# A hybrid decoder layer on one core: setup products as steps beside the first layer, exponents ordered behind copies of turned keys, attention rows' halves ordered behind the third convolution tile

## Chip, core and metric

The kernel runs on one core of a Trainium2 chip. The metric is the device time of one execution in microseconds (us). The engines are TensorE (PE, matrix products and transposes), VectorE (DVE), ScalarE (ACT), GpSimd (POOL) and SyncE (SP, which issues DMAs only). DMAs are also issued from ACT's and POOL's queues.

## What is computed

One layer for a prompt of 512 tokens and 8 samples of 8 tokens, 576 columns together:

```python
h = x + 0.5 * swiglu(rmsnorm(x, ffn1_norm), ...)          # D 1024, D_FF 2816
xn = rmsnorm(h, mix_norm)
z, xbc, dt, q, k, v, f, g_ssd, g_att = split_combined(xn @ w_in)
y_ssd = ssd_branch(z, xbc, dt, state_conv, state_ssm)     # causal conv of 4 taps on 3072 channels, scan, gate, norm
c = cumsum(logf)                                          # per head, over cached pages and new tokens
y_att = softmax(q k^T / 8 + c_q - c_k) v                  # 16 heads, 4 key heads; samples also see 2048 cached tokens
h = h + (sigmoid(g_ssd) * (y_ssd @ w_ssd_proj) + sigmoid(g_att) * (y_att @ w_attn_proj)) @ w_out
y = h + 0.5 * swiglu(rmsnorm(h, ffn2_norm), ...)
```

The inputs that the change touches are `state_conv` (the last three rows before the convolution, of each sample), `cache_logf` (logs of the forget gates in 160 pages, of which `page_table` names 128), and `state_ssm` (the scan's state).

## The kernel before

**Products.** Activations lie with features on partitions and the 576 tokens as columns, worked on in two halves of 288. Each fp32 product is made of three products in a faster format (`mm3`): a weight tile is split into a high part (`whi`, a copy on ACT, L173) and a low part (`wlo`, a difference on DVE or POOL, L174), and the activations into `xh` and `xl` in the same way; PE adds high by high (L208), high weight by low activation (L209) and low weight by high activation (L210). So a tile of 128 outputs by 288 columns over 1024 features is 24 matmuls. Weights come in stages of 512 KB on SP's queue, four of them in rotation.

**Order.** Each engine carries out its instructions in a fixed order. A scheduler sets it when the program is built: it goes by the order of the code, by a simulated time, and by `soon()`, which moves what is inside it ahead. During attention PE's order is written by hand (`manual_schedule`).

**The first layer.** `ffn` runs over 22 feature tiles in two parts (12 and 10): per tile four half products (96 matmuls), and after each part 8 output tiles. After each of these 38 steps it calls a generator named `beside`, which puts in a piece of other work. In the kernel before, that generator is `turns(4)`: after four steps, each step loads 256 KB of the scan's state on SP (L375), transposes it on PE (`tr`, L376), copies it on ACT (`hT`, L378) and stores it to DRAM (`hTD`).

**Setup.** In the code ahead of the first layer stand two small pieces. One loads the convolution rows (`sc`, L510), transposes them in 24 pieces (L515), copies them (`scT`, L516) and stores them to `scD` (L517). The other gathers the cached logs by page (`lg`, L524), runs 16 scans along the pages on DVE (`pf`, L529), collects their ends (`tot`, L531), multiplies them on PE by a matrix that sums over the earlier pages (L535), copies the result (`st`, L537), subtracts it in 16 instructions on POOL (L540), and stores the outcome to `pastD` in 32 DMAs on ACT's queue (L546). The state loads of `turns` take the memory that this piece leaves.

**Attention.** The loop takes 37 steps. In a step one key tile row of the prompt's pair of heads (`cur`) and one quarter of a sample's cached keys (`new`) are worked on. The pair's rows end in an exponent (`L`, ACT, L867), the first step of a pair with 512 columns, the others with fewer. The sample's keys are transposed on PE (L924) and copied on ACT (`kT`, L926); PE then multiplies them by the queries (L935). The results for the samples are collected in `ys` (DVE, L997) and at the end copied by POOL into the eight attention rows `qy` (L1114).

**Convolution.** `conv_tile` is called for the tiles B, C and X0 to X3 of a group of heads (`group_in`). It copies the stored rows into `xr` on POOL (L1129), runs the two half products, evicts them on DVE (L1133, L1138, L1140), transposes the last rows on PE into the free end of the second half's bank (L1146), copies that on ACT (`tt`, L1148), stores it, and works out the convolution (`kf`: ACT L1157, DVE L1159), its tanh (ACT, L1160) and the outputs (DVE). From here on two banks of PSUM serve the products. After the six tiles come the halves of the eight attention rows: `yh` on ACT (L217) and `yl` on DVE (L218), called from L1185, and then the projection of attention.

## Time and profile before

| | us |
|---|---|
| median of 3 runs | 1887.17 (1885.02, 1887.17, 1891.32) |
| the profiled execution | 1890.57 |
| its span in the trace | 1888.4 |
| PE busy | 1834.7 |
| DVE busy | 1062.6 |
| ACT busy | 746.2 |
| POOL busy | 606.5 |

The span is the time from the first to the last instruction of the profiled execution; what lies around it is 2.2 us. The page gives for each engine its busy time, which is a share of the span, and for a wait the engine and line that waited, the engine or DMA that ended the wait, and the total, the number and the longest. Numbers of buffers are left out of names in these views (`acc`, `whi`); in the rows of an order they stand behind the name. The granted clock is TensorE's, as a share of full speed.

### The profile page before, as it was taken

Reading aid. Unit: us, or ns where it says so; the run is one execution under the profiler, and the core shown is the slowest. Engines: PE = TensorE matmul, PEld = TensorE weight load, DVE = VectorE, ACT = ScalarE, POOL = GpSimd, SP = SyncE. Lnnn points to the kernel's source line nnn. Section 1 sums busy time; section 2 is a strip of 40 time slices with the busy share of each in tenths; the row PEclk is TensorE's granted clock in tenths of the full one; section 3 lists DMA queues with packets and bytes.
Section 4 is the critical chain, followed back from the end, with each engine's and each line's share of the span. In section 5 each row is a group of like instructions: output and inputs, shape, how many; then the busy total and the mean of one; then the engine's idle time right before and its main releaser. Section 6 shows DMA issues by size and latency. Waiting matters only on the chain.

```text
span 1888.4 us, 38769 instructions
## 1 busy us (share of the span) xinstructions
PE 1834.7 (97%) x15335; PEld 1729.5 (92%) x15335; DVE 1062.6 (56%) x2309; ACT 746.2 (40%) x1555; POOL 606.5 (32%) x681
## 2 busy tenths in 40 slices
PE   7999999999999999999999999999999999999998
PEld 7999999999889787888899898888989999999998
DVE  4544234434425677777655968787695544444442
ACT  4233223334323545545335645454433333223322
POOL 0432003322322344443323735656553332002210
PEclk9999999999999999999999999999999999999999
DMA  5453443445525678775456545354463444444432
GB/s 154 107 147 124 134 124 112 124 146 142 140 79 167 184 223 228 233 217 156 117 144 189 151 113 149 98 152 143 134 210 90 118 130 133 144 132 125 117 119 67
DMA packets 297722, 269.71 MB, mean 143 GB/s; under 512 B 55068, under 2 KB 262092, under 8 KB 297388
## 3 DMA queue, kind: packets, MB, share of 16 engines
q1 hardware_dynamic: 229712, 184.16, 34.9%
q10 hardware_dynamic: 57828, 46.10, 7.9%
q0 software_dynamic: 10000, 36.97, 6.3%
q8 instruction: 121, 1.98, 0.5%
q14 instruction: 61, 0.50, 0.1%
HBM read 223.72 MB, written 38.73 MB: 139 GB/s over the span
## 4 chain that ended last, share of the span: by engine, by line
PE 83%; DVE 7%; DMA 3%; ACT 3%; issue 2%; POOL 1%; ACTq 1%; SPq 0%; DVEq 0%; POOLq 0%
PE acc L208 16%; PE acc L209 16%; PE acc L210 15%; PE pv L209 8%; PE pv L208 8%; PE pv L210 7%; PE tr L935 2%; PE tr L924 1%; PE mm L861 1%; DMA ab<-cumD 1%; PE pv L892 1%; DVE kf L1159 1%; PE mm L879 1%; PE pv L973 1%; PE tr L376 1%
## 5 line engine op out<-in xcount | busy, mean ns | idle before, releaser
L173 ACT ACTIVATE whi<-stage 128x512 fp32r<-128x512 f32 (+2 forms) x474 | 294.7, 622 | 713.0 <-PE acc L209 605.2
L208 PE MATMUL acc<-xh,whi 128*128 128x288 f32 x1792 | 542.3, 303 | 8.4 <-ACT tt L1148 3.6
L209 PE MATMUL acc<-xl,whi 128*128 128x288 f32 x1792 | 533.8, 298 | 0.0
L210 PE MATMUL acc<-xh,wlo 128*128 128x288 f32 x1792 | 533.0, 298 | 0.0
L174 DVE TENSOR_TENSOR wlo<-stage,whi 128x512 fp32r<-128x512 f32 (+1 forms) x373 | 260.7, 699 | 268.1 <-ACT whi L173 251.1
L208 PEld LDWEIGHTS acc<-xh,whi 128*128 128x128 f32 x1792 | 339.5, 189 | 15.7 <-ACT tt L1148 7.7
L209 PEld LDWEIGHTS acc<-xl,whi 128*128 128x128 f32 x1792 | 339.7, 190 | 2.9 <-issue 2.7
L210 PEld LDWEIGHTS acc<-xh,wlo 128*128 128x128 f32 x1792 | 338.9, 189 | 1.1 <-issue 0.5
L174 POOL TENSOR_TENSOR wlo<-stage,whi 128x512 fp32r<-128x512 f32 (+1 forms) x101 | 138.4, 1370 | 287.7 <-ACT whi L173 275.5
L341 POOL TENSOR_TENSOR u<-u,s 128x288 f32<-128x288 f32 x88 | 81.5, 927 | 437.2 <-DVE u L340 379.8
L208 PE MATMUL pv<-xh,whi 128*128 128x288 f32 (+1 forms) x720 | 214.2, 298 | 1.7 <-ACT xh L220 1.5
L209 PE MATMUL pv<-xl,whi 128*128 128x288 f32 (+1 forms) x720 | 213.1, 296 | 0.0
L210 PE MATMUL pv<-xh,wlo 128*128 128x288 f32 (+1 forms) x720 | 212.6, 295 | 0.0
L208 PEld LDWEIGHTS pv<-xh,whi 128*128 128x128 f32 (+1 forms) x720 | 135.3, 188 | 2.3 <-ACT xh L220 1.8
L209 PEld LDWEIGHTS pv<-xl,whi 128*128 128x128 f32 (+1 forms) x720 | 135.1, 188 | 1.3
L210 PEld LDWEIGHTS pv<-xh,wlo 128*128 128x128 f32 (+1 forms) x720 | 135.2, 188 | 0.2
L208 PE MATMUL pv<-hh,whi 128*128 128x288 f32 x352 | 105.7, 300 | 0.0
L343 POOL TENSOR_TENSOR hl<-u,hh 128x288 fp32r<-128x288 f32 x88 | 79.4, 904 | 80.4 <-ACT hh L342 80.4
L209 PE MATMUL acc<-hl,whi 128*128 128x288 f32 x352 | 104.1, 296 | 0.0
L208 PE MATMUL acc<-hh,whi 128*128 128x288 f32 x352 | 104.1, 296 | 0.0
L209 PE MATMUL pv<-hl,whi 128*128 128x288 f32 x352 | 104.1, 296 | 0.0
L210 PE MATMUL acc<-hh,wlo 128*128 128x288 f32 x352 | 104.1, 296 | 0.0
(364 smaller groups left out, 3618.0 us busy)
## 6 DMA issues: line engine op xcount, KB each, us to landing
stage<-in_w_in_dram SPq DMA_DIRECT2D x52, 512.0 KB
stage<-in_ffn_w_up_dram SPq DMA_DIRECT2D x44, 512.0 KB
stage<-in_ffn_w_gate_dram SPq DMA_DIRECT2D x43, 512.0 KB
stage<-in_ffn_w_down_dram SPq DMA_DIRECT2D x40, 512.0 KB
h<-in_state_ssm_dram SPq DMA_DIRECT2D x64, 256.0 KB
hTD<-hT ACTq DMA_DIRECT2D x32, 256.0 KB
pb<-pastD SPq DMA_DIRECT2D x32, 256.0 KB
ab<-cumD SPq DMA_DIRECT2D x32, 256.0 KB
```

The source lines that it names most:

```text
L173: act(hi, view, AF.Copy)
L174: e.tensor_tensor(lo, view, hi.bitcast(F32), ALU.subtract)
L208: mm(out, lhsT=hi, rhs=a, start=first and i == 0, stop=False)
L209: mm(out, lhsT=hi, rhs=b, start=False, stop=False)
L210: mm(out, lhsT=lo, rhs=a, start=False, stop=last and i == n - 1)
L341: G.tensor_tensor(u, u, sil[half], ALU.mult)
L343: G.tensor_tensor(hl[:, hs(half)], u, hh[:, hs(half)].bitcast(F32), ALU.subtract)
L376: nc.tensor.transpose(ps[:, b * P:(b + 1) * P], h0[:, b, :], ident)
L861: mm(s[:, :n], lhsT=q, rhs=ks[2 * self.p + e][:, :n], start=hl == 0, stop=hl == 1)
L879: nc.tensor.transpose(t[:, j * P:(j + 1) * P], lt[:, j * P:(j + 1) * P], ident)
L892: mm(self.ob[o:o + 32, i * P:(i + 1) * P], lhsT=vtok[j][:, v0:v0 + 32], rhs=self.pts[e][:, j * P:(j + 1) * P], start=j == 0, stop=j == i)
L935: mm(s[kv * 32:(kv + 1) * 32, :], lhsT=self.q(kv), rhs=self.kT[kv // 2], start=True, stop=True)
```

## The change

It has three parts. Two tiles of the setup code become steps of a new generator `aside`, which runs beside the first layer: the loads of the convolution rows at the first call, their transposes after two more, then the gather and the scans, and after two further calls the matrix product, the subtractions and the stores; the state's turning follows as `turns(1)`, and its loads are issued up to three steps ahead. In attention, the exponents of a pair's first step are ordered behind both copies of the turned keys of the same step. After attention, the copies into the attention rows and their halves move behind `group_in`, where each of them is ordered behind an instruction of the third convolution tile, X0: POOL's copy behind X0's copy of the stored rows, ACT's `yh` behind X0's tanh, DVE's `yl` behind X0's last output. The tile `ys` moves to another pool for that. `behind` adds an order between two instructions, which the scheduler keeps.

```diff
+    def behind(later, first):
+        tc.add_manual_dep(later.ins, first.ins.name, ..., reason="order")
...
 def turns(wait):
+            tiles = []
             for t in range(16):
                 for h in range(2):
-                    h0 = tl(sp_, [P, 4, P], tag="h0", bufs=4)
-                    nc.sync.dma_start(out=h0, in_=ap3(A["state_ssm"][0], *place(h, t)))
+                    for n in range(len(tiles), min(2 * t + h + 3, 32)):
+                        tiles.append(tl(sp_, [P, 4, P], tag="h0", bufs=4))
+                        nc.sync.dma_start(out=tiles[n], in_=ap3(A["state_ssm"][0], *place(n % 2, n // 2)))
+                    if t + h == 0:
+                        yield
+                    h0 = tiles[2 * t + h]
...
+        def aside():
+            with pool("rows", side="right", reuse_waits="tile") as su:
+                sc = tl(su, [24, CONV], tag="sc")
...
+                yield
+                yield
+                scT = tl(su, [P, 24, 24], tag="scT")
...
+            with pool("lg", side="right", reuse_waits="tile") as lp:
...
+                for _ in range(2):
+                    yield
+                t = sm()
+                mm(t[:, :16], lhsT=page, rhs=tot, start=True, stop=True)
...
+            yield from turns(1)
...
-        ffn(nrm1, cg, A["ffn1_w_up"][0], A["ffn1_w_down"][0], hts, done1, turns(4))
+        ffn(nrm1, cg, A["ffn1_w_up"][0], A["ffn1_w_down"][0], hts, done1, aside())
...
-        ys = tl(ap, [P, 2, 4, NS], tag="ys")
+        ys = tl(yp, [P, 2, 4, NS], tag="ys")
...
-                    act(lt[:, :n], lt[:, :n], AF.Exp, bias=mn, scale=-1.0, accum_out=sum_)
+                    self.exps.append(act(lt[:, :n], lt[:, :n], AF.Exp, bias=mn, scale=-1.0, accum_out=sum_))
...
                     with soon():
-                        act(self.kT[p], t, AF.Copy)
+                        copy = act(self.kT[p], t, AF.Copy)
+                    for x in exps:
+                        behind(x, copy)
...
-                    new.turn_keys(jq)
+                    new.turn_keys(jq, cur.exps if jq == 0 else ())
...
-        for p in range(2):
-            for g in range(4):
-                G.tensor_copy(yt[p * 4 + g][:, NP:], ys[:, p, g, :])
...
-            yhl = [hilo(yhp, y, "yh", "yl", bufs=8) for y in yt]
+            yhl = []
+            for n, y in enumerate(yt):
+                c = G.tensor_copy(y[:, NP:], ys[:, n // 4, n % 4, :])
+                hi = tl(yhp, [P, NT], F32R, tag="yh", bufs=8)
+                lo = tl(yhp, [P, NT], F32R, tag="yl", bufs=8)
+                h = act(hi, y, AF.Copy)
+                for x, first in zip((c, h, V.tensor_tensor(lo, y, hi.bitcast(F32), ALU.subtract)), convs[2]):
+                    behind(x, first)
+                yhl.append((hi, lo))
```

How it moves instructions shows at three places. The first is on PE, in the first layer, around the transposes of the convolution rows; before:

```order
L208 MATMUL acc_706<-xh_203,whi_672 128x288
L209 MATMUL acc_706<-xl_204,whi_672 128x288
L210 MATMUL acc_706<-xh_203,wlo_673 128x288
L515 MATMUL tr_335<-ident_76,sc_330 128x24 x12
L515 MATMUL tr_349<-ident_76,sc_330 128x24 x12
L208 MATMUL acc_706<-xh_216,whi_672 128x288
L209 MATMUL acc_706<-xl_217,whi_672 128x288
L210 MATMUL acc_706<-xh_216,wlo_673 128x288
```

The same place of the program on PE with the change, where the line of the transposes is L530:

```order
L212 MATMUL acc_746<-xh_229,whi_712 128x288
L213 MATMUL acc_746<-xl_230,whi_712 128x288
L214 MATMUL acc_746<-xh_229,wlo_713 128x288
L530 MATMUL tr_777<-ident_76,sc_484 128x24 x12
L530 MATMUL tr_791<-ident_76,sc_484 128x24 x12
L212 MATMUL pv_845<-xh_138,whi_837 128x288
L213 MATMUL pv_845<-xl_139,whi_837 128x288
```

Before, the transposes stand inside the second feature tile's second product, behind 186 matmuls of 288 columns; now they stand between the third and the fourth tile, behind 288. The product of the totals (L535, now L551) has 480 such matmuls ahead of it instead of 312, and the first state transposes (L376, now L385) 734 instead of 555; between the two are 254 instead of 243. On DVE, with the change, the scans (L543) and what stands behind them read as follows.

```order
L344 TENSOR_TENSOR u_940<-pv_915,rbc_262 128x288
L543 SCALAR_TENSOR_TENSOR pf_814<-cst_75,lg_812 128x128 x16
L178 TENSOR_TENSOR wlo_1056<-stage_1051,whi_1055 128x512
L344 TENSOR_TENSOR u_970<-acc_945,rbc_262 128x288
L178 TENSOR_TENSOR wlo_1060<-stage_1053,whi_1059 128x512
L545 COPY tot_831<-pf_814 128x16
```

Before, an eviction (`u`) stood between the fourteenth and the fifteenth scan; now all sixteen stand together, ahead of a weight's low part, which PE first reads at its matmul number 435.

The second place is on ACT, at the first step of a pair in attention; before (`Ls` and `Ln` are the samples' exponents, `L` the pair's, `kT` the copies of turned keys):

```order
L951 ACTIVATE Ls_7380,sums_7389<-Ls_7380,mxs_6934 128x512
L952 ACTIVATE Ln_7387,sums_7389<-Ln_7387,mxs_6934 128x64
L867 ACTIVATE L_7418,sum_7421<-L_7418,mn_7419 128x512
L867 ACTIVATE L_7429,sum_7432<-L_7429,mn_7430 128x512
L926 ACTIVATE kT_7458<-tr_7459 128x512
L926 ACTIVATE kT_7465<-tr_7466 128x512
L896 ACTIVATE qy_7504<-pv_7149 128x512
```

And on ACT with the change (L944 are the copies, L884 the pair's exponents):

```order
L971 ACTIVATE Ls_7384,sums_7393<-Ls_7384,mxs_6938 128x512
L972 ACTIVATE Ln_7391,sums_7393<-Ln_7391,mxs_6938 128x64
L944 ACTIVATE kT_7462<-tr_7463 128x512
L944 ACTIVATE kT_7469<-tr_7470 128x512
L884 ACTIVATE L_7422,sum_7425<-L_7422,mn_7423 128x512
L884 ACTIVATE L_7433,sum_7436<-L_7433,mn_7434 128x512
L913 ACTIVATE qy_7508<-pv_7153 128x512
```

Here the two copies and the two exponents have changed places.

The third place is the convolution. On POOL before, from the copies into the attention rows to the copies of stored rows for the tiles X0 (`xr_11790`), B (`xr_11622`) and C (`xr_11706`):

```order
L1114 COPY qy_7504<-ys_6513 128x64
L174 TENSOR_TENSOR wlo_11787<-stage_11780,whi_11786 128x512
L1114 COPY qy_8067<-ys_6513 128x64
L1114 COPY qy_8633<-ys_6513 128x64
L1114 COPY qy_9199<-ys_6513 128x64
L1114 COPY qy_9765<-ys_6513 128x64
L1114 COPY qy_10331<-ys_6513 128x64
L1114 COPY qy_10897<-ys_6513 128x64
L1114 COPY qy_11386<-ys_6513 128x64
```

On POOL with the change, the tiles are `xr_11786` (X0), `xr_11618` (B) and `xr_11702` (C):

```order
L178 TENSOR_TENSOR wlo_11783<-stage_11776,whi_11782 128x512
L1145 COPY xr_11786<-scT_11602 128x8x3
L1207 COPY qy_7508<-ys_6517 128x64
L1207 COPY qy_8071<-ys_6517 128x64
L1207 COPY qy_8637<-ys_6517 128x64
L1207 COPY qy_9203<-ys_6517 128x64
L1207 COPY qy_9769<-ys_6517 128x64
L1145 COPY xr_11618<-scT_11602 128x8x3
L1145 COPY xr_11702<-scT_11602 128x8x3
L1207 COPY qy_10335<-ys_6517 128x64
```

Before, all eight copies of rows stand ahead of the three copies of stored rows; now five do ahead of those of B and C. On ACT with the change, the eight halves stand between X0's tanh (L1176) and the work for tile X1 (`xr_11865`, `kf_11928`, `tt_11922`), where no other work stood before; there they followed the last copies of attention, ahead of tile B's `kf`:

```order
L1176 ACTIVATE xr_11786<-kf_11849 128x600
L1210 ACTIVATE yh_12102<-qy_7508 128x576
L1210 ACTIVATE yh_12107<-qy_8071 128x576
L1210 ACTIVATE yh_12112<-qy_8637 128x576
L1210 ACTIVATE yh_12117<-qy_9203 128x576
L1210 ACTIVATE yh_12122<-qy_9769 128x576
L1210 ACTIVATE yh_12127<-qy_10335 128x576
L1210 ACTIVATE yh_12132<-qy_10901 128x576
L1210 ACTIVATE yh_12137<-qy_11390 128x576
L177 ACTIVATE whi_12023<-stage_11938 128x512
L1173 ACTIVATE kf_11928<-xr_11865,P_31_125,P_80_293 128x600
L1164 ACTIVATE tt_11922<-acc_11894 91x128
```

All eight now delay, on ACT, the weight's high part `whi_12023`, X1's first product and the copy that frees X1's bank. `yl` on DVE has moved likewise, behind X0's last output.

## Prediction

> **What bounds the kernel now.** I read first the page's busy shares, then the waits of TensorE, then its stretches, then the chain of waits and the timeline at the places that the change touches.

> ```profile
> PE 1834.7 (97%) x15335; PEld 1729.5 (92%) x15335; DVE 1062.6 (56%) x2309; ACT 746.2 (40%) x1555; POOL 606.5 (32%) x681
> ```

> TensorE (PE) is busy for 1834.7 of the span's 1888.4 us. Its instructions stay the same in number and shape, so the change can win only from the 53.7 us in which PE idles, and from time in which it works slowly. The waits of PE (total us, times, longest) that end at lines of the change:

> ```profile
> PE tr L935 <- ACT kT L926: 5.2, 6, 1.1
> PE tr L376 <- DMA h<-in_state_ssm_dram: 2.8, 1, 2.8
> PE tr L515 <- DMA sc<-in_state_conv_dram: 1.8, 1, 1.8
> PE mm L535 <- DVE tot L531: 1.3, 1, 1.3
> ```

> Together 11.1 us. The slow work shows in the stretches (start:end, length, then busy us and count of PE, PEld, DVE, ACT and POOL, the granted clock, the DMA share, GB/s):

> ```profile
> 50.00:60.00 10.00, 10.00 (x76) 9.97 (x76) 4.79 (x9) 2.67 (x6) 5.98 (x7) 0.83 0.21 48
> 100.00:110.00 10.00, 7.16 (x45) 6.95 (x44) 5.97 (x10) 4.15 (x10) 7.13 (x8) 0.85 0.68 190
> 110.00:120.00 10.00, 10.00 (x76) 10.00 (x76) 4.87 (x9) 4.39 (x8) 2.09 (x2) 0.98 0.28 88
> 200.00:300.00 100.00, 100.00 (x764) 100.00 (x763) 33.17 (x58) 27.70 (x48) 7.68 (x8) 1.00 0.43 131
> 920.00:930.00 10.00, 6.96 (x39) 6.54 (x39) 8.19 (x13) 6.40 (x12) 3.46 (x11) 0.83 0.02 3
> 1150.00:1160.00 10.00, 7.72 (x83) 6.62 (x82) 9.86 (x17) 6.67 (x20) 6.49 (x7) 1.00 0.60 128
> ...
> 53.10 0.24 PE pv L208
> ```

> In the undisturbed stretch a matmul costs 100/764 = 0.131 us. The granted clock drops just behind three of the places: (1 - 0.83) x 10 = **1.7 us** is lost in 50 to 60, (1 - 0.85) x 10 + (1 - 0.98) x 10 = 1.7 us from 100 to 120, and 1.7 us in 920 to 930. In the last row, of the chain of waits, a matmul there takes 0.24 us. So some PE gaps are paid twice: once idle, once in a slow stretch of half the rate behind them. Not all are: the stretch at 1150 has 2.3 us of idle time at clock 1.00, and none follows the 1.3 us wait on the totals. I take it that 1.8 us or more close together can bring the drop, and 1.3 us does not.

> **Part 1, the setup work beside FFN1.** The chain of waits (start, us, what), from the transposes of the convolution rows over the gather of the cached logs to the first turned state; the row of the scans is from DVE's timeline:

> ```profile
> 49.79 1.63 PE tr L515 x24
> ...
> 57.49 6.20 DMA lg<-in_cache_logf_dram,pcol
> ...
> 63.72 4.53 DVE L529 TENSOR_TENSOR_SCAN pf<-cst,lg 128x128 f32<-128x128 f32 x14 [1.77 <-DMA lg<-in_cache_logf_dram,pcol]
> ...
> 70.35 0.76 DVE tot L531
> ...
> 74.08 7.07 POOL lg L540 x16
> ...
> 81.17 0.35 ACTq L546
> ...
> 98.67 4.70 DMA pastD<-lg
> 103.63 2.92 DMA h<-in_state_ssm_dram
> 106.69 0.87 PE tr L376 x4
> ```

> The order shows 288 half-width matmuls ahead of the 24 transposes of the convolution rows, where there were 186. The 102 more cover 13 us, against a wait of 1.8 us: that gap goes. With it I expect its slow stretch to go. The matrix product of the totals stands behind 480 such matmuls, formerly 312: 192 behind the transposes instead of 126, 8.6 us more, so the 1.33 us wait on the totals goes too.

> The state transposes don't get free in the same way. From the product (71.16, just after the totals' copy ended) to the first state transposes (106.69) the chain takes 35.5 us: 16 subtractions on POOL, 32 stores issued from ACT's queue, their landing, and the state load that waits for the stores because it takes their memory. Nothing shortens it; the prefetch puts more loads in flight but the first still waits. PE had 243 matmuls in that time and idled 2.84 us; now it has 254, 11 more, worth 1.44 us. What is left is 2.84 - 1.44 = 1.4 us, below what brought a drop. Sum of part 1: 1.8 + 1.7 + 1.33 + 1.44 + 1.7 = **8.0 us** gained. Bounds: if both slow stretches stay, 4.6; if the chain gets covered whole, 9.4.

> What is queued behind the added steps: DVE has all 16 scans in a row, 16 x 4.53/14 = 5.2 us, and they block it while the gather is out. In before the gather landed 12.3 us after the transposes' end (51.4 to 63.7), 94 matmuls' worth: 288 + 94 = 382. The scans end at matmul 382 + 40 = 422, the next low part of a weight (0.7 us, 5 matmuls) at 427, and PE reads it at its 435th. Spare: 8 matmuls, 1 us. I cost it at nothing; the rival below prices the cover's loss. On SP's queue six state loads move behind the stage loads of two later steps; those loads were already there and PE does not wait for either.

> **Part 2, exponents behind the copies of turned keys.** The timeline of ACT and PE in one step (the last row from the chain of waits):

> ```profile
> 650.91 0.33 ACT L952 ACTIVATE Ln<-Ln,mxs 128x64 f32<-128x64 f32 x1
> ...
> 651.24 0.71 ACT L867 ACTIVATE L<-L,mn 128x512 f32<-128x512 f32 x1
> ...
> 651.95 0.71 ACT L867 ACTIVATE L<-L,mn 128x512 f32<-128x512 f32 x1
> ...
> 652.65 1.05 ACT L926 ACTIVATE kT<-tr 128x512 f32<-128x512 f32 x2
> ...
> 649.47 1.04 PE L924 MATMUL tr<-ident,kk 128*128 128x128 f32 x8
> ...
> 653.27 1.10 PE L935 MATMUL tr<-kT,qz 128*32 128x512 f32 x6 [0.96 <-ACT kT L926]
> ...
> 658.83 0.87 PE mm L879 x8
> ```

> The keys are turned by 650.5, but the copies stand behind two exponents of 0.71 us, 1.41 with their accumulator reads. Taken ahead, they start at 651.24 and the first ends near 651.8, before PE's other work ran out at 652.3. PE idled 0.96 here and 5.2 us at six such places; the gain is **5.0 us** (3.5 if the copy still ends late where a gap was 0.7 to 1.1, 5.3 with the small wait of the same kind). The exponents end 1.05 us later, at 653.8 instead of 652.7; PE turns their results from 658.83 on, with a division on DVE between, so I cost that at nothing. If that cover were gone, it would be 1.05 x 6 = 6.3 us lost.

> **Part 3, attention rows' halves behind X0.** Where the convolution begins:

> ```profile
> 917.09 0.46 DVE L997 COPY ys<-tr 64x64 f32<-64x64 f32 x2 [0.49 <-PE tr L990]
> ...
> 918.18 0.37 PE L208 MATMUL acc<-xh,whi 128*128 128x288 f32 x1 [1.13 <-DVE xr L1133]
> ...
> 922.83 0.35 PE L1146 MATMUL acc<-ident,xr 128*91 128x128 f32 x1 [1.25 <-POOL xr L1129]
> 924.96 0.40 PE L208 MATMUL acc<-xh,whi 128*128 128x288 f32 x1 [1.78 <-ACT tt L1148]
> ...
> 917.82 1.28 POOL L174 TENSOR_TENSOR wlo<-stage,whi 128x512 fp32r<-128x512 f32 x1
> 919.05 2.36 POOL L1114 COPY qy<-ys 128x64 f32<-128x64 f32 x7
> ...
> 921.46 2.00 POOL L1129 COPY xr<-scT 128x24 f32<-128x24 f32 x3
> ...
> 919.84 4.13 ACT L217 ACTIVATE yh<-qy 128x576 fp32r<-128x576 f32 x7 [1.28 <-POOL qy L1114]
> 923.88 0.87 ACT L1157 ACTIVATE kf<-xr,P,P 128x600 f32<-128x600 f32 x1
> ...
> 944.09 0.63 ACT L173 ACTIVATE whi<-stage 128x512 fp32r<-128x512 f32 x1 [0.26 <-PE acc L209]
> 944.78 0.89 ACT L1157 ACTIVATE kf<-xr,P,P 128x600 f32<-128x600 f32 x1
> 947.44 0.27 ACT L1148 ACTIVATE tt<-acc 91x128 f32<-91x128 f32 x1 [1.77 <-PE acc L1146]
> ```

> The first gap (1.13) falls to about 0.1: DVE's eviction stood behind two copies of sample rows that wait for PE's transposes (917.09), and in the new order it comes ahead of them. For the second the order is POOL's: after the weight part, X0's copy (2.00/3 = 0.67), five row copies (5 x 0.3) and only then tile B's own copy: 919.0 + 0.67 + 1.5 + 0.67 = 921.8, 1.0 us sooner than 922.8, and PE too comes 1.0 sooner; the gap stays about 1.15. The third falls to about 0.85, since ACT's seven halves are gone. Gain 1.03 + 0.1 + 0.93 = 2.06 us, and the slow stretch, 1.7, goes as well.

> But the eight halves (8 x 4.13/7 = 4.7 us of ACT) now stand between X0's tanh and what tile X1 needs: a weight's high part, its first product (kf) and the copy tt that frees its accumulator. In the later steady tile ACT had 0.26 + 1.77 = 2.0 us idle at that place, and 0.1 between. So tt comes 4.7 - 2.1 = 2.6 us late, and PE, which waits for the bank, idles 2.6 us there. By the rows above a gap of that size brings a slow stretch of 1.7. Net: 2.06 + 1.7 - 2.6 - 1.7 = **-0.5 us**, a loss. Bounds: 3.8 gained if nothing waits (the halves slip into other slack), 4.3 lost if the first gaps stay and the new one comes.

> **The sum.** 8.0 + 5.0 - 0.5 = 12.5 us. The profiled execution took 1890.57 us, so 1878.1 by it; that execution lay 3.4 above the median of the runs, 1887.17, from which the sum gives 1874.7. I take a value between: **1876 us**.

> [...] By the rows, drops of the clock follow gaps of 1.8 and 2.84 us. [...]

> **Rivals.**
> - *The drops aren't caused by these gaps* and stay or come elsewhere: no slow stretch is won or lost. 1.8 + 1.33 + 1.44 + 5.0 + 2.06 - 2.6 = 9.0 us, so 1878 from the median, 1881.5 from the profiled execution: about **1880**. For it: a gap at 1150 brought none. Against: three drops directly behind gaps. Chance 0.2. [...]
> - *The halves hide fully behind X0*: no new stall in part 3, and the gain there is 3.8; 16.8 us in all, about **1872**. For it: ACT is busy 40% of the span. Against: the order has eight in a row ahead of tt. Chance 0.2.
> - *The attention gain is replaced*: another wait at the same step ends as late (scores of the pair wait for their exponents). Then part 2 gives 0 to 2: about **1880**. For it: the six places have ACT full for 5 us. Against: PE's readers come 5 us after the exponents' new end. Chance 0.1.
> - *The late gather, on the slower side*: DVE stands in order behind the scans until the gather lands, so PE runs out of weight parts. It decides from 1 us of lateness on; each further us of landing costs PE one. In the trace the gather took 6.2 us where the DMA share was 0.21; in 100 to 110 the share is 0.68, so it can meet more traffic. To lose 12.5 + 5.7 us it would have to land 19 us late, 25 us in all: **1893** and above. Chance 0.05.
> - *The change doesn't do what it says*, a moved step being ordered back: the order shows all three moves, so 0.02, at 1887.

> **How the numbers follow.** My forecast has 0.43. What a measurement of this kernel can tell from no change is about 0.3%, 5.7 us: faster is below 1881.5. The forecast and the full hiding lie below it; of the two cases near 1880, two thirds do: faster 0.83. Within: 0.13. Slower: 0.04, all from the gather. The range reaches from full hiding with its upper bounds (9.4 + 5.3 + 3.8 = 18.5 from the median, 1868.7) to the 1880 cases with a part of the losses that the lower bounds of parts 1 and 3 allow (3.4 and 3.8 us below their terms): **1868 to 1885**.

> **What would show it.** Right: no PE wait on sc or tot; one of about 1.4 us on the first h; none on kT; clock 1.00 at 50 to 60 and 100 to 120; a PE wait on tt of X1 of about 2.6 us some 25 to 30 us into the convolution. Wrong: a wait on a weight's low part at 65 to 75; a longer wait on h; waits on L where kT's were; no wait on tt, with the halves hidden; drops of the clock that stay though their gaps are gone.

## The result and the profile after

The changed kernel took 1869.12 us (median of 4 runs, 1867.37 to 1872.9); the kernel before 1887.72 us (median of 4). The ratio is 0.9903, with a 95% interval of 0.988 to 0.9926: **18.6 us by the medians, 14.0 to 22.7 by the interval**. The prediction was 1876 us, in a range of 1868 to 1885, and its sum 12.5 us. The profiled execution of the change took 1870.09 us, with a span of 1868.2. Ratios here and below leave out one execution of the study, of the kernel with the halves alone, which took 2210.41 us at a granted clock of 0.752.

The busy shares, then the waits of PE in total, in the profile of the change:

```profile
PE 1824.8 (98%) x15335; PEld 1725.6 (92%) x15335; DVE 1064.6 (57%) x2309; ACT 742.1 (40%) x1555; POOL 605.7 (32%) x681
...
PE acc L212 <- DVE xr L1149: 4.0, 3, 1.8
PE tr L385 <- DMA h<-in_state_ssm_dram: 2.6, 1, 2.6
PE acc L1162 <- DVE xr L1156: 1.6, 2, 1.0
```

The same number of PE instructions is busy for 9.9 us less, and PE idles 43.4 us instead of 53.7. The waits on `sc`, on the totals and on `kT` are gone; the wait on the first state load stayed (2.6 instead of 2.8); the waits on DVE's evictions in the convolution (L1149, L1156) are longer (5.6 together instead of 3.5), those on ACT's copy `tt` shorter (1.5 instead of 3.8). So of the span's 20.2 us some 10 lie in idle time, and as much in time that counts as busy. One part of that is the slow stretches. The granted clock (third number from the end) in the stretches that answer to those of before:

```profile
50.00:60.00 10.00, 10.00 (x77) 9.84 (x76) 6.30 (x11) 3.72 (x9) 5.33 (x6) 1.00 0.34 107
100.00:110.00 10.00, 10.00 (x78) 10.00 (x77) 3.47 (x6) 2.39 (x4) 0.81 (x1) 1.00 0.51 60
120.00:130.00 10.00, 7.35 (x45) 7.15 (x44) 4.95 (x8) 4.16 (x9) 4.06 (x6) 0.83 0.65 201
930.00:940.00 10.00, 8.17 (x49) 7.75 (x48) 7.95 (x15) 4.50 (x7) 2.10 (x3) 0.83 0.12 31
```

The drop at 50 is gone, which is worth 1.7 us; the ones behind the first state load and in the convolution have moved with their waits. Another part of the "busy" gain is in attention. In PE's timeline with the change, and in ACT's, the step that the prediction showed of before:

```profile
641.46 1.04 PE L942 MATMUL tr<-ident,kk 128*128 128x128 f32 x8
...
644.22 1.15 PE L955 MATMUL tr<-kT,qz 128*32 128x512 f32 x8
...
645.53 0.97 PE L878 MATMUL mm<-Ks,qs 128*128 128x384 f32 x4
...
643.22 1.05 ACT L944 ACTIVATE kT<-tr 128x512 f32<-128x512 f32 x2
644.17 0.71 ACT L884 ACTIVATE L<-L,mn 128x512 f32<-128x512 f32 x1
```

From the key transposes to the next products of the prompt's scores (L878) PE takes 4.07 us. Before, the same way ran from 649.47 to 654.95, in this row of PE's timeline of before:

```profile
654.95 0.97 PE L861 MATMUL mm<-Ks,qs 128*128 128x384 f32 x4
```

That is 5.48 us, 1.41 more, of which the waits had listed 0.96.

### The profile page after: what moved, and what is told of

Read it like the earlier page. It is cut to its first block, busy times and chain, and to the rows that moved or that the text cites. A ratio compares the mean times of both kernels' runs of the same rounds, so it can differ in the third digit from the quotient of the medians.

```text
span 1868.2 us, 38772 instructions
## 1 busy us (share of the span) xinstructions
PE 1824.8 (98%) x15335; PEld 1725.6 (92%) x15335; DVE 1064.6 (57%) x2309; ACT 742.1 (40%) x1555; POOL 605.7 (32%) x681
## 4 chain that ended last, share of the span: by engine, by line
PE 63%; DVE 7%; ACT 1%; DMA 1%; issue 1%; POOL 0%; ACTq 0%; SPq 0%; DVEq 0%; POOLq 0%
PE acc L212 13%; PE acc L214 12%; PE acc L213 12%; PE pv L213 4%; PE pv L214 4%; PE pv L212 4%; PE tr L955 2%; PE tr L942 2%; PE mm L878 1%; DMA ab<-cumD 1%; PE pv L909 1%; PE mm L896 1%; DVE kf L1175 1%; PE tr L982 1%; PE pv L993 1%
```

## The experiments

**Each part alone.** Three kernels are the one before with one part of the diff each; a fourth has only the line of part 3 that moves the tile `ys` to the other pool:

```diff
-        ys = tl(ap, [P, 2, 4, NS], tag="ys")
+        ys = tl(yp, [P, 2, 4, NS], tag="ys")
```

Setup alone:

> Part 1 alone: the setup work beside the first layer, nothing else changed. Theory of the prediction: 8.0 us faster than before (no wait on the convolution rows or the totals, 1.4 us of wait on the first state load, two slow stretches gone). Theory from the trace of the change: 5.5 us, with 2.6 us of wait on the first state load and a slow stretch behind it; the waits on the copies of turned keys stay at 5.2 us over six places, and those on the copies of sample rows at 1.6. Rival: if the attention stage gets shorter here too, the gain of attention has to do with what the moved setup leaves (memory, code position), not with the exponents.

Exponents alone, in two sittings:

> Part 2 alone: the exponents of a pair's first step ordered behind the copies of turned keys. Theory of the prediction: 5.0 us faster than before, the idle time that the trace lists at six places. Theory from the trace of the change: 11 to 12 us, since each of seven first steps of a pair gets 1.25 to 1.46 us shorter (also the part of the stall that lies inside busy rows), and the waits on the copies of sample rows (1.6 us at steps just before) go too. Rival: 9 to 10 us, when only the first steps get shorter and the rest belongs to another part or to the one profiled execution.

> Part 2 alone once more, beside the run with one copy moved. Theory of the prediction: 5.0 us faster than before. Theory of the hidden second wait: 5.6 us at the start of the products and 2.8 us inside the row, 8.4 us faster than before; first products 2.77 us behind the key transposes and 1.30 and 2.05 from there to the next.

Halves alone, and the pool alone:

> Part 3 alone: attention rows' halves behind the third convolution tile, with the collecting tile in another pool. Theory of the prediction: 0.5 us slower than before (3.8 won at the start of the convolution, 2.6 of new wait and 1.7 of a slow stretch at the fourth and fifth tile). Theory from the trace of the change: 0.5 to 1 us faster, with 3.9 us of waits and 1.5 of a slow stretch won and about 4.9 lost on evictions of DVE that stand behind the halves' lower parts. Rival: 3 to 4 us faster, when the new waits come only with the other parts' timing. The waits of attention stay as before.

> Only the tile that collects the sample rows moves to the other pool; copies and halves stay where they were. It moves one pair of copies on DVE behind the first tile's evictions. Theory: the first wait of the convolution (1.13 us) goes and nothing else, about 1 us faster, not to be told from no change. [...]

| kernel | ratio to before (95%) | us gained |
|---|---|---|
| setup alone | 0.9951 (0.9935 to 0.9967) | 9.3 (6.2 to 12.3) |
| exponents alone | 0.9959 (0.9944 to 0.9975) | 7.8 (4.7 to 10.6) |
| exponents alone, again | 0.9955 (0.9941 to 0.997) | 8.5 (5.7 to 11.1) |
| halves alone | 0.9991 (0.9973 to 1.0008) | 1.7 (-1.5 to 5.1) |
| pool alone | 0.9973 (0.9957 to 0.9989) | 5.1 (2.1 to 8.1) |

Gains are the ratio's distance from 1 times the median of before in that sitting (1890.83, and 1885.5 for the repeat). The three parts add within their intervals: 9.3 + 7.8 + 1.7 = 18.8 us, as much as the whole change. By the medians of the same executions they are 6.5, 7.4 and 1.6, together 15.4, so the sum is no closer than that. My expectation of 11 to 12 us for the exponents, read from one trace, lies above the first interval and at the upper end of the repeat's; the prediction's 5.0 is inside the first and below the repeat's. The pool alone did better than its expectation of about 1 us, by the ratio; by the medians it gained 2.2. Waits of PE from 905 to 960 us, first in the kernel with the pool alone, then in that with the halves moved as well:

```profile
PE acc L208 <- DVE xr L1133: 1.3, 1, 1.3
PE acc L208 <- ACT tt L1148: 1.0, 3, 0.5
...
PE acc L212 <- DVE xr L1133: 2.1, 2, 1.7
PE acc L1146 <- DVE xr L1140: 1.0, 1, 1.0
PE mm L1314 <- DVE xg L1163: 0.8, 1, 0.8
PE acc L212 <- ACT tt L1148: 0.6, 2, 0.4
```

Before, this stretch had 5.1 us of waits. With the pool alone 2.3 us are left of them, with the halves behind the third tile 4.5. The pool takes the eviction past the sample rows' copies, which stood ahead of it before; DVE's rows with the pool alone:

```profile
920.03 0.45 DVE L1133 TENSOR_TENSOR xr<-acc,rbc 128x288 f32<-128x288 f32 x1
...
920.93 0.45 DVE L997 COPY ys<-tr 64x64 f32<-64x64 f32 x2
```

The tie of the halves trades the waits at the start for others.

**Where the exponents' gain lies.** The prediction took the idle time that the waits list. The rival reading was that PE waits twice, for each copy of turned keys, and that the second wait lies inside a row counted as busy. This kernel moves only the first copy ahead, and ties the second behind both exponents:

```diff
-                    for x in exps:
-                        behind(x, copy)
+                    if p == 0:
+                        for x in exps:
+                            behind(x, copy)
+                    elif exps:
+                        behind(copy, exps[-1])
```

> Against the kernel before, only the first of the two copies of turned keys moves ahead of the pair's two exponents; the second stays behind them. Theory of the prediction (the idle time that the view of waits lists, 5.2 us, is the whole cost, and it ends with the first copy): 5 us faster than before. Theory of the hidden second wait (products with the second copy stand in a row counted as busy and wait for it too): the first products start 0.8 to 1.0 us sooner, at 2.77 us behind the key transposes instead of 3.5 to 3.9, but the stretch from there to the next products grows by as much, from 1.7 and 2.5 to about 2.5 and 3.4, since the second copy ends when it did; 0 to 1 us faster than before.

The ratio was 1.0024 (1.0013 to 1.0035): 4.5 us slower. PE's timeline of this kernel at the same step, and ACT's:

```profile
652.33 1.04 PE L929 MATMUL tr<-ident,kk 128*128 128x128 f32 x8
...
655.10 1.05 PE L945 MATMUL tr<-kT,qz 128*32 128x512 f32 x4
656.62 0.62 PE L945 MATMUL tr<-kT,qz 128*32 128x512 f32 x2 [0.47 <-ACT kT L931]
...
657.82 0.97 PE L865 MATMUL mm<-Ks,qs 128*128 128x384 f32 x4
...
654.10 0.58 ACT L931 ACTIVATE kT<-tr 128x512 f32<-128x512 f32 x1
...
655.99 0.58 ACT L931 ACTIVATE kT<-tr 128x512 f32<-128x512 f32 x1
```

The first products start 2.77 us behind the key transposes, as in the change (2.76); the second half waits for the second copy, and the way to L865 is 5.49 us, as before. So taking away the wait ahead of the first products gained nothing, because the second copy sets when the step goes on. The prediction's reading, that the idle time listed there is the whole cost, is refuted. The idle time itself is not gone from the list of this kernel; much of it shows at another place:

```profile
PE tr L945 <- ACT kT L931: 4.8, 8, 2.2
...
626.25 1.05 PE L945 MATMUL tr<-kT,qz 128*32 128x512 f32 x4 [2.23 <-ACT kT L931]
```

The size of the gain comes from the same rows at seven first steps of a pair. The kernel before spent 25.0 us from the key transposes to the first products; the change, where nothing else disturbs a step, takes 7 x 2.77 = 19.4: 5.6 us. From there to the next products it was 16.4 instead of 1.31 + 6 x 2.04 = 13.6: 2.8 us. Together 8.4, against 7.8 and 8.5 measured.

That the kernel came out 4.5 us slower, not level, has its likely reason in the first step of the whole loop, which the seven leave out. There the second copy stood between the two exponents before; now it stands behind the second, which itself waits for DVE, and PE waits 2.23 us for it (the row above). The whole step takes 7.78 us instead of 5.27. Two more steps are 1.2 us longer each: one has a new wait on DVE, and at the other, in the fourth pair, PE had not waited before. That makes 4.8 us, in one profile. The runs also had a lower mean granted clock, 0.9929 against 0.9941, an estimated 2.3 us of 1885, so the account is not exact.

**The convolution and the first state load.** Four kernels ran together: the change again; the change with the halves left where they had stood (parts 1, 2 and the pool); the halves tied two to a tile; and the state's turning one call later:

```diff
-                for x, first in zip((c, h, V.tensor_tensor(lo, y, hi.bitcast(F32), ALU.subtract)), convs[2]):
+                for x, first in zip((c, h, V.tensor_tensor(lo, y, hi.bitcast(F32), ALU.subtract)), convs[1 + n // 2]):
...
-            yield from turns(1)
+            yield from turns(2)
```

> The changed kernel itself, for comparison with the next three on one chip. From its first runs: ratio 0.990 to the kernel before, 18.6 us. If the three parts add, 9.3 + 7.7 + 1.7 = 18.7 us by the ratios of the three runs with one part each.

> Parts 1 and 2, and of part 3 only the other pool: the halves stand where they stood before, not behind the third convolution tile. Theory: the pool alone takes the waits at the convolution's start down from 4.2 to 1.9 us and the slow stretch behind them, and the order behind the third tile gives 3.2 us of waits and a slow stretch back; so this is 2 to 4 us faster than the changed kernel. Rival (the tie is what wins): 2 to 4 us slower than the changed kernel.

> The changed kernel with the halves tied two each behind the second to the fifth convolution tile, instead of all eight behind the third. Theory that eight in a row are too much for the slack of a tile (2.0 us on ACT, less on DVE): two take 1.2 us on ACT and 1.4 on DVE, the waits at the fourth and fifth tile (3.5 us) and the slow stretch (1.7) go, so 3 to 5 us faster than the changed kernel. Rival: DVE has no slack of 1.4 us in a tile and each tile waits a little: no difference.

> The changed kernel with the turning of the state one step later: 34 more matmuls, 4.5 us, ahead of the first state transposes, and 32 turns that end one call after the last step. Theory that the chain of stores is 2.6 us longer than its cover: the wait on the first state load (2.6 us) and the slow stretch behind it (1.7) go, 4 us faster than the changed kernel. Rival by which the slow stretch does not hang on the wait: 2.6 us. Rival by which the last turn costs at the end: no difference.

| kernel | ratio to before (95%) | median, us |
|---|---|---|
| the change again | 0.9897 (0.988 to 0.9915) | 1873.01 |
| halves where they stood, new pool | 0.9891 (0.9875 to 0.9908) | 1871.25 |
| halves spread | 0.9882 (0.9865 to 0.9898) | 1869.79 |
| turning one call later | 0.9887 (0.987 to 0.9903) | 1870.18 |

All intervals overlap: no single one is told apart from the change by its time, and the gains of 2 to 5 us that I expected of the last three are neither shown nor excluded. With the new pool and the halves where they stood the time is the same as with part 3 whole, so no run shows that the tie of the halves wins anything. The traces show what each does. With the halves spread, the waits at the fourth and fifth tile are gone, and two of 1.4 us together come in the projection. With the turning one call later the wait on the first state load and the drop behind it are gone:

```profile
120.00:130.00 10.00, 10.00 (x79) 10.00 (x78) 5.98 (x9) 4.69 (x10) 6.72 (x7) 1.00 0.64 188
```

Both together ran beside the change once more:

> The changed kernel with the halves tied two each behind the second to the fifth convolution tile, and the turning of the state one step later. If the two add to what their runs showed in the trace (waits of 3.5 us and a slow stretch of 1.7 gone for 1.5 us of new waits; 2.6 us and a slow stretch of 1.7 gone): 5 to 8 us faster than the changed kernel. Rival, from the two runs' times (2.8 and 1.9 us): 3 to 5 us.

> The changed kernel once more, for comparison with the run before it on one chip: ratio 0.990 to the kernel before. If the waits on the copies of sample rows (none in its first trace, 1.6 us in its second) belong to single executions, either may show here.

They took 0.9875 (0.9855 to 0.9896), median 1861.85 us, where the change took 0.9919 (0.9902 to 0.9935), median 1870.21: 8.4 us faster than the change by the medians, where 5 to 8 had been expected, with intervals that don't meet. This is the fastest kernel of the study.

## Why the prediction was right, and where it was off

The direction and the range held, though the time lies only 1.1 us above the range's lower end, and the sum was 6 us too small. All three terms came out larger than forecast. Step by step:

**Setup: the mechanism right, one term wrong, and some luck.** 8.0 us was forecast, 9.3 measured (6.2 to 12.3). The waits on `sc` and the totals went, as argued, and the scans did not starve PE: the rival of the late gather did not come. The step "nothing shortens the chain, so 1.4 us of wait are left" failed: the wait is 2.65 us, with a drop of the clock behind it, because the chain grew, from 35.5 to 36.7 us (87.23, the product, to 123.90). POOL's and ACT's timelines of the change, and PE's row of the first state transposes:

```profile
90.57 6.39 POOL L556 TENSOR_TENSOR lg<-pf,st 128x128 f32<-128x128 f32 x14
96.92 0.81 POOL L347 TENSOR_TENSOR hl<-u,hh 128x288 fp32r<-128x288 f32 x1
97.68 0.76 POOL L556 TENSOR_TENSOR lg<-pf,st 128x128 f32<-128x128 f32 x2
98.47 2.88 ACTq L562 DMA_DIRECT2D pastD<-lg  x6
...
87.23 0.29 PE L551 MATMUL mm<-tot,page 128*128 128x16 f32 x2
...
123.90 0.90 PE L385 MATMUL tr<-ident,h 128*128 128x128 f32 x4 [2.65 <-DMA h<-in_state_ssm_dram]
```

One of the layer's own products stands between the subtractions, and they start 3.3 us behind the matrix product instead of 2.9: 1.2 us more up to the first store, as large as the miss. The 9.3 us are made up otherwise than forecast. The waits gave 3.3 us instead of 4.6. For the slow stretches the granted clock of all executions tells more than one trace: its mean is 0.9953 with the setup alone and 0.9935 before, in the same sitting, an estimated 3.4 us of 1885, as much as the two stretches of the sum. Another 1.5 us lie where the prediction did not look, in the first step of attention's loop: from the key transposes over the first products to the next ones it takes 2.80 + 0.99 us in the kernel with the setup alone, 3.51 + 1.76 before. The 2.80 shows in all eight traces with the setup part and in none of the six without. This gain made up for the missing 1.25 us of cover, and that is luck.

**Exponents: the mechanism right, the size too small.** The term was 5.0 us with an upper bound of 5.3, and 8.4 was there to be had. The mis-sized term is "PE idled 0.96 here and 5.2 us at six such places". It left out the second wait in each step, 2.8 us in all, and 0.4 us by which the way to the first products was longer than the listed waits. The rival, another wait that ends as late, did not come at most steps. In part it did: in the first and the third profile of the change one set of key transposes waits for DVE's copies of the samples' turned exponents (`PTs`), which the trace of before doesn't show, and the step takes 3.9 to 4.1 us to its first products instead of 2.77:

```profile
PE tr L942 <- DVE PTs L984: 0.9, 1, 0.9
```

The second profile of the change has no such wait; the two profiles with the exponents alone have 1.2 and 1.7 us of it.

**Halves: the sign of the new wait right, its place wrong.** A loss of 0.5 us was forecast, a gain of 1.7 (-1.5 to 5.1) measured. The mis-sized term is the gain at the start: of 4.2 us of waits the prediction left 2.1 standing, and 0.8 is left. New waits came at the fourth and fifth tile, but not because ACT's copy `tt` was late. PE's, DVE's and ACT's timelines of the change:

```profile
924.11 0.40 PE L212 MATMUL acc<-xh,whi 128*128 128x288 f32 x1 [1.70 <-DVE xr L1149]
931.74 0.35 PE L1162 MATMUL acc<-ident,xr 128*91 128x128 f32 x1 [1.01 <-DVE xr L1156]
932.91 0.30 PE L1330 MATMUL mm<-ident,xg 128*64 128x128 f32 x1 [0.82 <-DVE xg L1179]
...
920.25 3.44 DVE L1211 TENSOR_TENSOR yl<-qy,yh 128x576 fp32r<-128x576 f32 x5
923.61 0.45 DVE L1149 TENSOR_TENSOR xr<-acc,rbc 128x288 f32<-128x288 f32 x1
923.98 3.18 DVE L1211 TENSOR_TENSOR yl<-qy,yh 128x576 fp32r<-128x576 f32 x3
...
918.65 4.69 ACT L1210 ACTIVATE yh<-qy 128x576 fp32r<-128x576 f32 x8
```

Five low parts on DVE stand ahead of the eviction that frees the bank; three more, and the products behind them, ahead of the next. The waits there are 1.70 + 1.01 + 0.82 = 3.5 us, where 2.6 was forecast. That the eight in a row are what costs, the kernel with the halves spread shows in its trace; "full hiding" was not what happened. The drop of the clock forecast behind these waits came in the first profile of the change, and not in the second and third.

**The slow stretches: not settled by the length of a gap.** I had taken a gap of 1.8 us or more as their cause. In the change the first state load's wait of 2.65 us has a drop behind it; in the third profile of the same kernel a longer wait has none:

```profile
124.75 0.63 PE L385 MATMUL tr<-ident,h 128*128 128x128 f32 x4 [3.01 <-DMA h<-in_state_ssm_dram]
...
120.00:130.00 10.00, 6.99 (x55) 6.78 (x54) 5.75 (x10) 4.36 (x10) 5.30 (x6) 1.00 0.71 209
```

```profile
120.71:124.12 3.41, 0.76 (x7) 1.00 0.74 226
124.12:127.54 3.42, 3.42 (x17) 0.50 0.82 246
...
119.59:123.00 3.41, 2.15 (x17) 1.00 0.78 225
123.00:126.41 3.41, 1.66 (x14) 1.00 0.83 236
126.41:129.83 3.42, 3.42 (x28) 1.00 0.54 159
```

The wait of 2.65 us lies whole in one step, and the next step runs at half the clock; the longer wait is shared by two steps, in which PE is busy for 63% and 49%, and none follows. The grid's place against the start of the span differs between executions of one program: these two lie 1.12 us apart (120.71 and 119.59). Counted over all traces, for steps at full clock from 20 us on: PE busy for less than 44% of a step brought a drop in 26 of 26 cases, 44 to 52% in 13 of 27, 52 to 60% in none of 13. Above that there are 16 drops in some 7400 steps. Of these, 14 are one in each trace at 580 to 592 us, behind products over 24 partitions and no gap (before, PE is busy for the whole 3.42 us of the step ahead of the drop at 591.63); the other two, one of them the drop at 52.32 us before, with PE busy for 74% of the step ahead, stand behind the 24 transposes of convolution rows. So busy time as the profile counts it is not all that matters.

## What to carry to other kernels

Idle time that a profile lists for a wait was a lower bound here (0.96 us listed in the step shown, whose way was 1.41 shorter with the change), where a group of instructions waits for several inputs: measure from one fixed instruction to the next one behind the group, on both sides of the change. Work that is moved off one engine's path goes onto the others' queues with all its parts; eight small instructions in a row cost what two to a stage did not (waits of 3.5 us, against two of 1.4 together). Price the slow stretch behind a short gap as a chance (one came behind 2.65 us, none behind 3.01 in the same program), and read the granted clock of all executions for it, not of one. And where a moved piece ends in a chain of stores and loads, count the cover behind it first: one more step of distance took the remaining wait of 2.65 us away.

## What the runs showed that I had not expected

Single executions of one program differ in attention. In the first profile of the change PE never waits for the copies of sample rows; in the second it does, with the same instructions:

```profile
PE tr L942 <- DVE ys L1017: 1.6, 5, 0.4
```

The third profile has none again. So about 2 us that seemed to be won in the first trace belonged to the execution. This is one reason why the first trace's attention (252.8 us from the first key transposes to the last, 266.1 before) overstated what the runs measured for the exponents, some 8 us; the loop's first step, which the setup part shortens too, is another. And a pool's name in one line, which changes no instruction, moved DVE's copies behind the evictions through the order that the scheduler then made, and gained 5.1 us (2.1 to 8.1) alone.
